# Attention transposes in the score slots' second banks, and the last two heads divided after the values

## The chip, the cores and the metric

The kernel runs on one core of a Trainium2 chip. The metric is the device time of one execution in microseconds. The core has a matrix engine (TensorE; PE in the profile, and PEld for its weight loads), a vector engine (DVE), a scalar engine (ACT) and a general engine (POOL). SyncE (SP) issues the transfers. Each engine works through its own instructions in a fixed order and waits on semaphores of the others. Matrix products land in PSUM, an accumulator memory that this kernel uses as eight banks of 512 fp32 numbers for each of 128 partitions.

## The reference, cut to what matters

The model is a two-layer trunk on a sequence of 1024 tokens with 1024 features: a forgetting attention, a SwiGLU block, a state-space mixer and another SwiGLU block, each between two RMS norms. The change touches the attention alone, which has 16 heads of 64 features:

```
for blk in range(seq_len // Q_BLOCK):            # 8 blocks of 128 queries
    s = jnp.einsum('bhqd,bhkd->bhqk', qb, kb).astype(jnp.float32) * scale
    s = s + c[:, :, q0:k_end, None] - c[:, :, None, :k_end]
    s = jnp.where(mask, s, -jnp.inf)
    p = jax.nn.softmax(s, axis=-1).astype(vb.dtype)
    outs.append(jnp.einsum('bhqk,bhkd->bhqd', p, vb))
o = o * jax.nn.sigmoid(gate)
return o @ w_out
```

The softmax is a quotient: the exponentials may be divided by their row sums before they meet the values, or the output of the values may be divided afterwards. Both give the same numbers up to rounding.

## The kernel before, in words

The attention is worked in **units**: one head `h` and one block of 128 queries `qb`. The blocks of a head run from 7 down to 0, and block `qb` sees `(qb + 1) * 128` keys, so the first four units of a head (qb 7 to 4) have more than 512 keys and the last four have 512 or fewer. There are 128 units.

**`scores(h, qb)`** (L542 on) adds the causal mask to one square of the bias tile on POOL (L547) and takes a score slot with `self.S("S")`. There are two slots, taken in turn, each of two PSUM banks: banks 0 and 1, banks 2 and 3. Unit i and unit i + 2 therefore have the same slot. TensorE fills it (L551 and L552, in pieces of 512 keys, so only units with qb of 4 or more write the second bank). DVE adds the bias in place and takes the row minimum (L555). ACT takes the exponential into an SBUF page `Pt` and the row sums into a column of `rs` (L561). For the last two heads (14 and 15, the pair called hp 7) DVE inverts the row sum (L563) and POOL multiplies the whole of `Pt` by it (L564).

**`transposes(h, qb)`** (L576 on) turns `Pt` over in squares of 128, up to four squares to a **group**: units with qb of 4 or more have two groups, the others one, so a head has 12 groups and a pair of heads 24. A group's squares are transposed by TensorE into one PSUM bank (L588), copied by ACT as the high part `pth` (L591) and subtracted by DVE to give the low part `ptl` (L592). The bank comes from `self.pb(PTB, ...)`. `PTB` has one entry, bank 6, so all groups of all units go through this bank, one after another.

**`values(h, j)`** (L594 on) multiplies two units' transposed squares with the values into bank 7 (L607). Every second time it copies and adds the two halves into the output page `o` (L611, L612). At a pair's end, for the pairs 0 to 6, POOL multiplies the page by a page of inverse sums (L614). Those come from **`sums(hp)`** (L566 on): the 16 columns of row sums are transposed through bank 6 (L569), inverted by DVE on 16 partitions (L570), written to DRAM and read back repeated over 64 partitions (L571, L573). Pair 7 has no such step.

**`attend`** strings the units together: in step i the scores of unit i, the transposes of unit i - 1 and, every second step, the values of two units before. **`fox`** weaves this stream with other matrix work of the same time: while the attention of pair hp runs, the projections q, k and v of pair hp + 1 and the gate of pair hp - 1 (L272 to L274, called `fm`) are handed out in shares. For hp 7 there are no projections left: what runs beside it is the gate of pair 6, the split of the first four output weights, the gate of pair 7 and the first tiles of `out_proj` (the same lines L272 to L274 with `woh` and `wol`). `out_proj` takes its accumulators with `self.S("pso")` from the same two slots.

The gate (L510 on) multiplies `o` with the sigmoid of the gate projection (L522). For pairs 0 to 6 the result goes to DRAM and comes back as the operand of `out_proj`. For pair 7 it stays in SBUF (`ogk`) and is split there (`wh`, `wl`, L253 and L254). It is the last of the eight k steps of each output tile.

The order of each engine's instructions is fixed when the kernel is built. A planner hands out the instructions by priority, which is their place in the program unless a block raises it (`high_priority(AHEAD)` around L555) or lowers it (the weight splits, L253 and L254). An instruction that the planner holds for not ready, by its own estimates of durations, is passed over, and a later one takes its place. So the transposes stand in the midst of `fm` products where the planner expects the bank to be free. Dependences in PSUM are kept bank by bank; the planner adds the semaphores.

Of the kernel before, what the change touches and what calls it, by code (L numbers as in the profile page):

```python
# [12 lines left out]
ALU = mybir.AluOpType  # L13

P = 128
D = 1024
NT = 8
NH = 16
HD = 64
# [12 lines left out]
PTB = (2,)  # L32
# [3 lines left out]
def f32(ap):  # L36
    return ap.bitcast(F32)
# [121 lines left out]
class Trunk:  # L159
# [369 lines left out]
    def attend(self, c, o):  # L529

        nc = self.nc
        units = [(h, qb) for h in range(NH) for qb in reversed(range(8))]
        An, pt, Pt, pv, rs, ri = {}, {}, {}, {}, {}, {}

        def load_bias(h):
            An[h] = self.R("An")
            nc.sync.dma_start(An[h], self.bcast(self.csum[h:h + 1, :], D))  # L540

        def scores(h, qb):  # L542
            qh, ql = c[h // 2]["q"][h % 2 * 2:h % 2 * 2 + 2]
            k = c[h // 2]["k"][h % 2]
            nk = (qb + 1) * P
            qs = slice(qb * P, nk)
            nc.gpsimd.tensor_add(An[h][:, qs], An[h][:, qs], self.cmask)  # L547
            ps = self.S("S")
            for c0 in range(0, nk, 512):
                c1 = min(c0 + 512, nk)  # L550
                nc.tensor.matmul(ps[:, c0:c1], qh[:, qs], k[:, c0:c1], start=True, stop=False)  # L551
                nc.tensor.matmul(ps[:, c0:c1], ql[:, qs], k[:, c0:c1], start=False, stop=True)  # L552
            with self.tc.high_priority(AHEAD):
                m = self.small("mx")
                nc.vector.tensor_tensor_reduce(out=ps[:, :nk], in0=ps[:, :nk], in1=An[h][:, :nk], op0=ALU.add, op1=ALU.min,  # L555
                                               scale=1.0, scalar=3e38, accum_out=m)
            p = Pt[h, qb] = self.R("Pt")
            if h // 2 not in rs:
                rs[h // 2] = self.small("rs", (P, 2, 8))
            r = rs[h // 2][:, h % 2, qb:qb + 1]  # L560
            nc.scalar.activation(p[:, :nk], ps[:, :nk], AF.Exp, bias=m, scale=-1.0, accum_out=r)  # L561
            if h >= NH - 2:
                nc.vector.reciprocal(r, r)  # L563
                nc.gpsimd.tensor_scalar(p[:, :nk], p[:, :nk], r, 1.0, op0=ALU.mult, op1=ALU.mult)  # L564

        def sums(hp):  # L566

            p2, r, x = self.pb(PTB, (P, P))[0:16], self.small("ri", (16, P)), self.R("RI")
            nc.tensor.transpose(p2, rs.pop(hp).rearrange("p a b -> p (a b)"), self.ident)  # L569
            nc.vector.reciprocal(r, p2)  # L570
            nc.sync.dma_start(self.ri_d[hp], r)  # L571
            for i in range(2):
                nc.sync.dma_start(x[i * 64:i * 64 + 64], self.bcast(self.ri_d[hp][i * 8:i * 8 + 8], D, 64))  # L573
            ri[hp] = x

        def transposes(h, qb):  # L576
            j, qq = qb // 2, qb % 2
            if qq:
                ng = (2 * j + 2 + 3) // 4
                pt[h, j] = [(self.R("pth", (P, 4, 256), F32R), self.R("ptl", (P, 4, 256), F32R)) for _ in range(ng)]  # L580
            p = Pt.pop((h, qb))
            for g in range(0, qb + 1, 4):
                n = min(4, qb + 1 - g)
                if g:
                    yield 0.11 * 4
                p2 = self.pb(PTB, (P, 4, P))
                for i in range(n):
                    nc.tensor.transpose(p2[:, i], p[:, (g + i) * P:(g + i + 1) * P], self.ident)  # L588
                th, tl = pt[h, j][g // 4]
                dh, dl = th[:, 0:n, qq * P:qq * P + P], tl[:, 0:n, qq * P:qq * P + P]  # L590
                nc.scalar.copy(dh, p2[:, 0:n])  # L591
                nc.vector.tensor_sub(dl, p2[:, 0:n], f32(dh))  # L592

        def values(h, j):  # L594
            h2, vt = h % 2, c[h // 2]["v"]
            if h2 == 0 and j == 3:
                o[h // 2] = self.R("o")
            r = slice(h2 * 64, h2 * 64 + 64)
            if j % 2:
                pv[h] = self.pb(PVB)  # L600
            out = pv[h][:, (j % 2) * 256:(j % 2) * 256 + 256]
            last = 2 * j + 1
            t = pt.pop((h, j))
            seq = [(0, 0)] + [(kb, i) for kb in range(1, last + 1) for i in (0, 1)] + [(0, 1)]
            for n, (kb, i) in enumerate(seq):
                lo = P if kb == last else 0
                nc.tensor.matmul(out[:, lo:], vt[kb // 4][:, kb % 4, h2, :], t[kb // 4][i][:, kb % 4, lo:],  # L607
                                 start=(n == 0), stop=(n == len(seq) - 1))
            if j % 2 == 0:
                d = o[h // 2][r, (j // 2) * 512:(j // 2) * 512 + 512]  # L610
                nc.scalar.copy(d, pv[h][64 - h2 * 64:128 - h2 * 64])  # L611
                nc.vector.tensor_add(d, d, pv[h][r])  # L612
                if h2 and j == 0 and h < NH - 2:
                    nc.gpsimd.tensor_mul(o[h // 2], o[h // 2], ri.pop(h // 2))  # L614

        load_bias(0)
        for i in range(len(units) + 3):
            hp = min(i, len(units) - 1) // 16
            if i < len(units):
                h, qb = units[i]  # L620
                if qb == 7:
                    yield 0.0, hp
                scores(h, qb)
                if qb == 2 and h + 1 < NH:
                    load_bias(h + 1)
                yield 0.16 * (qb + 1), hp
            if 1 <= i <= len(units):
                h, qb = units[i - 1]
                for x in transposes(h, qb):
                    yield x, hp  # L630
                yield 0.11 * (qb % 4 + 1), hp
                if h % 2 and qb == 0 and h < NH - 2:
                    sums(h // 2)
            if i >= 3 and (i - 3) % 2 == 1:
                h, qb = units[i - 3]
                values(h, qb // 2)
                yield 0.22 * (qb + 1), hp
# [1066 lines left out]
```

## Time and profile before

| | us |
|---|---|
| median of 3 runs | 2428.12 (2426.31 to 2430.02) |
| the profiled execution | 2426.33 |
| its span, first to last instruction | 2424.5 |
| attention, from the first scores (70.4) to the last values (669.7) | about 599 |
| one pair of heads, pairs 1 to 6 | 77.3 to 77.6 |

A profile page gives the busy time of each engine, the chain of work that ended last and the costliest groups of instructions. `L588` is line 588 of the kernel, `ps<-ident,Pt` says that `ps` is written from `ident` and `Pt`, and `x576` counts instructions. In a timeline a row begins with its start and its duration in us, and the part in brackets is the idle time of that engine just before it and what ended it. Matrix products are pipelined: the next one starts before the last has ended, so the time that a wait takes from TensorE is read from one start to the next. Weight loads (PEld) run ahead of the products, and a load that waits delays its product only by what the load was not ahead.

### The profile page before, as it was taken

What the parts mean: (1) busy time and instruction counts of PE and PEld (TensorE: products, weight loads), DVE (VectorE), ACT (ScalarE), POOL (GpSimd) and SP (SyncE); (2) the same over time, 40 slices, a digit from 0 to 9 for tenths busy, and PEclk for the clock granted to TensorE, in tenths of its full rate; (3) what the DMA queues carried; (4) which work ended last, traced back from release to release, by engine and by line L of the source; (5) the groups of instructions that cost most, each with busy time, mean ns of one, the idle gap of its engine ahead of it and who ended that gap; (6) DMA issues with size and microseconds to landing.
All of it is one profiled execution on the core that took longest, in us unless ns stands there. A gap on an engine that the chain in (4) does not pass through costs nothing.

```text
span 2424.5 us, 31559 instructions
## 1 busy us (share of the span) xinstructions
PE 2359.3 (97%) x11683; PEld 1938.8 (80%) x11683; DVE 1689.1 (70%) x2684; ACT 1204.4 (50%) x2029; POOL 455.2 (19%) x427
## 2 busy tenths in 40 slices
PE   7999999999999999999999999999999999999997
PEld 5777778777777888888878779888878888888886
DVE  6867776677678967666668686763795656555867
ACT  6766676667646333434564563232453333333334
POOL 4222222222400034545520001410000000000003
PEclk9999999999999999999999999999999999999999
DMA  4121112121243444343688752443424333237874
GB/s 146 48 61 53 49 48 62 53 61 54 87 149 101 121 127 135 117 136 116 204 293 301 270 170 84 135 147 107 135 80 135 107 98 109 92 118 261 284 239 157
DMA packets 252427, 318.23 MB, mean 131 GB/s; under 512 B 34225, under 2 KB 179937, under 8 KB 252273
## 3 DMA queue, kind: packets, MB, share of 16 engines
q1 hardware_dynamic: 252272, 316.23, 40.9%
q8 instruction: 91, 1.49, 0.3%
q14 instruction: 64, 0.52, 0.1%
HBM read 238.46 MB, written 77.72 MB: 130 GB/s over the span
## 4 chain that ended last, share of the span: by engine, by line
PE 74%; DVE 12%; ACT 7%; DMA 3%; issue 3%; POOL 0%; SPq 0%; DVEq 0%; ACTq 0%; POOLq 0%
PE ps L841 33%; PE ps L943 10%; PE ps L272 7%; PE ps L274 7%; PE ps L273 7%; PE ps L588 2%; PE ps L607 2%; DVE ps L555 1%; DMA raw<-in_ffn_w_down_dram 1%; DMA rot_d<-ry 1%; ACT wh L253 1%; PE ps L552 1%; PE ps L551 1%; DVE ptl L592 1%; DVE y L318 1%
## 5 line engine op out<-in xcount | busy, mean ns | idle before, releaser
L841 PE MATMUL ps<-B,ah 128*128 128x512 f32 x1056 | 326.0, 390 | 0.3 <-ACT B L89 0.3
L943 PE MATMUL ps<-wdh,gh 128*128 128x512 f32 x616 | 241.4, 392 | 6.3 <-ACT m L962 3.7
L943 PE MATMUL ps<-wdh,gl 128*128 128x512 f32 x616 | 240.9, 391 | 1.9 <-DVE gl L254 1.9
L943 PE MATMUL ps<-wdl,gh 128*128 128x512 f32 x616 | 240.9, 391 | 0.8 <-DVE wdl L254 0.8
L841 PEld LDWEIGHTS ps<-B,ah 128*128 128x128 f32 x1056 | 198.1, 188 | 42.7 <-ACT B L89 1.2
L841 PE MATMUL ps<-ops,ah 128*128 128x512 f32 x704 | 218.2, 391 | 0.0
L272 PE MATMUL ps<-hT,wh 128*128 128x512 f32 x512 | 207.5, 406 | 1.3 <-DVE pt L429 0.7
L841 PE MATMUL ps<-B,al 128*128 128x512 f32 x528 | 205.4, 389 | 0.0
L273 PE MATMUL ps<-hT,wh 128*128 128x512 f32 x512 | 204.4, 399 | 0.0
L274 PE MATMUL ps<-hT,wl 128*128 128x512 f32 x512 | 202.6, 396 | 0.0
L253 ACT CAST gh<-gr 128x1024 fp32r<-128x1024 f32 (+1 forms) x78 | 81.1, 1040 | 166.4 <-PE ps L943 138.0
L592 DVE TENSOR_TENSOR ptl<-ps,pth 128x512 fp32r<-128x512 f32 x192 | 106.4, 554 | 78.6 <-ACT pth L591 73.6
L254 DVE TENSOR_TENSOR gl<-gr,gh 128x1024 fp32r<-128x1024 f32 (+1 forms) x78 | 98.3, 1262 | 84.0 <-ACT gh L253 83.7
L841 PEld LDWEIGHTS ps<-ops,ah 128*128 128x128 f32 x704 | 131.5, 188 | 28.7 <-issue 1.7
L812 DVE TENSOR_TENSOR al<-raw,ah 128x1024 fp32r<-128x1024 f32 x88 | 117.1, 1333 | 50.5 <-ACT ah L811 50.5
L1655 POOL TENSOR_TENSOR y<-m,s 128x512 f32<-128x512 f32 x4 | 6.5, 1628 | 764.3 <-DVE wdl L254 759.5
L547 POOL TENSOR_TENSOR An<-An,cmask 128x128 f32<-128x128 f32 x128 | 80.2, 629 | 365.8 <-DVE mx L555 332.3
L811 ACT CAST ah<-raw 128x1024 fp32r<-128x1024 f32 x88 | 92.6, 1052 | 101.8 <-PE ps L841 99.4
L943 PEld LDWEIGHTS ps<-wdh,gh 128*128 128x128 f32 x616 | 116.3, 189 | 32.8 <-ACT m L962 4.2
L943 PEld LDWEIGHTS ps<-wdh,gl 128*128 128x128 f32 x616 | 116.2, 189 | 26.9 <-DVE gl L254 2.7
L841 PE MATMUL ps<-ops,al 128*128 128x512 f32 x352 | 136.9, 389 | 0.0
L943 PEld LDWEIGHTS ps<-wdl,gh 128*128 128x128 f32 x616 | 116.3, 189 | 25.5 <-DVE wdl L254 1.5
(358 smaller groups left out, 5867.2 us busy)
## 6 DMA issues: line engine op xcount, KB each, us to landing
raw<-in_ffn_w_down_dram SPq DMA_DIRECT2D x98, 512.0 KB, 5.2
gr<-g_d SPq DMA_DIRECT2D x76, 512.0 KB, 4.4
raw<-in_ffn_w_gate_dram SPq DMA_DIRECT2D x44, 512.0 KB, 4.1
raw<-in_ffn_w_up_dram SPq DMA_DIRECT2D x44, 512.0 KB, 4.8
g_d<-s SPq DMA_DIRECT2D x66, 256.0 KB, 2.2
raw<-in_fox_w_in_dram SPq DMA_DIRECT2D x32, 512.0 KB, 4.3
g_d<-up SPq DMA_DIRECT2D x22, 512.0 KB, 2.7
g_d<-up SPq DMA_DIRECT2D x44, 256.0 KB, 2.9
```

The source lines that it names most:

```text
L253: self.nc.scalar.copy(h, src)
L254: self.lsub.tensor_sub(l, src, f32(h))
L272: mm(ps, lh, rh, start=start, stop=False)
L273: mm(ps, lh, rl, start=False, stop=False)
L274: mm(ps, ll, rh, start=False, stop=stop)
L547: nc.gpsimd.tensor_add(An[h][:, qs], An[h][:, qs], self.cmask)
L588: nc.tensor.transpose(p2[:, i], p[:, (g + i) * P:(g + i + 1) * P], self.ident)
L592: nc.vector.tensor_sub(dl, p2[:, 0:n], f32(dh))
L811: nc.scalar.copy(h, src)
L812: V.tensor_sub(l, src, f32(h))
L841: nc.tensor.matmul(bank, x[:, k], y, start=start and k == i == 0, stop=True, skip_group_check=True)
L943: nc.tensor.matmul(bank, x[:, j, t], y[:, j], start=start and i == 0, stop=True, skip_group_check=True)
```

## The change

**Part one.** Each unit remembers the second bank of its score slot (`own`). The unit's first group of transposes goes into that bank if the unit has qb of 2 or more; second groups, and the single groups of qb 1 and 0, go through bank 6 as they did.

**Part two.** For heads 14 and 15 the inversion L563 and the POOL multiplication L564 are gone, and `sums` is called for pair 7 too. There it inverts the sums on 16 partitions as for the other pairs, but sends nothing to DRAM: POOL writes a selection matrix of ones and zeros (two copies, 16 partitions of 512 numbers each), and eight products of 128 x 128 spread the inverse sums over the 128 partitions into a score slot (`self.S("ri", ...)`, both banks). After the last values of head 15, DVE multiplies the page `o` by it out of PSUM. Since `ri` takes a turn of the two slots, the accumulators of `out_proj` that follow swap slots.

```diff
@@ attend, scores
             ps = self.S("S")
+            own[h, qb] = self.slots[self.nS % len(self.slots)] + 1
...
             nc.scalar.activation(p[:, :nk], ps[:, :nk], AF.Exp, bias=m, scale=-1.0, accum_out=r)
-            if h >= NH - 2:
-                nc.vector.reciprocal(r, r)
-                nc.gpsimd.tensor_scalar(p[:, :nk], p[:, :nk], r, 1.0, op0=ALU.mult, op1=ALU.mult)
@@ sums
             nc.vector.reciprocal(r, p2)
+            if hp == NH // 2 - 1:
+                sel, ri[hp] = x[0:16].rearrange("p (q f) -> p q f", f=P), self.S("ri", (P, 8, P))
+                for i in range(2):
+                    nc.gpsimd.tensor_copy(sel[:, :, i * HD:i * HD + HD],
+                                          self.ident[0:16, i * 8:i * 8 + 8, None].to_broadcast([16, 8, HD]))
+                for qb in range(8):
+                    nc.tensor.matmul(ri[hp][:, qb], sel[:, qb], r, start=True, stop=True)
+                return
@@ transposes
-            p = Pt.pop((h, qb))
+            p, b = Pt.pop((h, qb)), own.pop((h, qb))
...
-                p2 = self.pb(PTB, (P, 4, P))
+                p2 = self.bank(b, 1, (P, 4, P)) if not g and qb > 1 else self.pb(PTB, (P, 4, P))
@@ values
-                if h2 and j == 0 and h < NH - 2:
-                    nc.gpsimd.tensor_mul(o[h // 2], o[h // 2], ri.pop(h // 2))
+                if h2 and j == 0:
+                    if h < NH - 1:
+                        nc.gpsimd.tensor_mul(o[h // 2], o[h // 2], ri.pop(h // 2))
+                    else:
+                        nc.vector.tensor_mul(o[h // 2], o[h // 2], ri.pop(h // 2).rearrange("p a b -> p (a b)"))
@@ the loop over units
-                if h % 2 and qb == 0 and h < NH - 2:
+                if h % 2 and qb == 0:
                     sums(h // 2)
```

More of the change, by code (lines that the diff above doesn't have):

```diff
@@ L535, in attend @@
         units = [(h, qb) for h in range(NH) for qb in reversed(range(8))]
-        An, pt, Pt, pv, rs, ri = {}, {}, {}, {}, {}, {}
+        An, pt, Pt, pv, rs, ri, own = {}, {}, {}, {}, {}, {}, {}
         def load_bias(h):
```

## The prediction

> **What bounds the kernel now.** I read the profile's page first, then the sums of busy time by stretch, the waits of TensorE in the attention, and the timeline at the waits.
>
> ```profile
> span 2424.5 us, 31559 instructions
> PE 2359.3 (97%) x11683; PEld 1938.8 (80%) x11683; DVE 1689.1 (70%) x2684; ACT 1204.4 (50%) x2029; POOL 455.2 (19%) x427
> ```
> ```profile
> 448.20:525.66 77.46, 75.85 (x412) 61.51 (x410) 55.64 (x97) 53.47 (x102) 18.63 (x25) 1.00 0.19 55
> 603.00:672.00 69.00, 65.79 (x358) 51.14 (x359) 47.35 (x94) 45.72 (x85) 25.20 (x32) 1.00 0.35 104
> ```
>
> TensorE sets the pace: 97% of the span, 75.85 of 77.46 us in a middle pair of heads, at the full granted clock (1.00; the rows give stretch, length, and the busy time of PE, PEld, DVE, ACT and POOL). DVE (55.64) and ACT (53.47) have over 20 us to spare there. So a change pays only by what it takes from TensorE: work, or moments in which TensorE waits. These are its waits over the whole attention (60.5 to 672 us), the array's first, the weight loader's below, with the total, the count and the longest:
>
> ```profile
> PE ps L588 <- DVE ptl L592: 8.5, 22, 0.6
> PE ps L588 <- POOL Pt L564: 0.8, 2, 0.4
> PEld ps L588 <- DVE ptl L592: 39.9, 99, 1.1
> ```
>
> The largest is the transposes waiting for DVE's subtraction of the group before, that is, for bank 6 to come free. What one such wait costs is read from start to start:
>
> ```profile
> 465.24 0.39 PE L274 MATMUL ps<-hT,wl 128*128 128x512 f32 x1
> 465.47 0.39 PE L272 MATMUL ps<-hT,wh 128*128 128x512 f32 x1
> 466.14 0.55 PE L588 MATMUL ps<-ident,Pt 128*128 128x128 f32 x3 [0.29 <-DVE ptl L592]
> ...
> 468.84 0.39 PE L272 MATMUL ps<-hT,wh 128*128 128x512 f32 x1
> 469.32 0.66 PE L588 MATMUL ps<-ident,Pt 128*128 128x128 f32 x4
> ...
> 512.63 0.39 PE L272 MATMUL ps<-hT,wh 128*128 128x512 f32 x1
> 513.60 0.33 PE L588 MATMUL ps<-ident,Pt 128*128 128x128 f32 x1 [0.58 <-DVE ptl L592]
> ```
>
> A 512-column product takes the array 0.23 us (465.24 to 465.47). From 512.63 to 513.60 are 0.97, so 0.74 are lost where the row says 0.58; from 465.47 to 466.14 are 0.67, so 0.44 where it says 0.29. A counted wait costs its idle time and 0.16. At 468.84 to 469.32 0.25 us are lost with no idle time counted at all.
>
> In the last pair the bank is the chain itself:
>
> ```profile
> 656.61 0.69 DVE L592 TENSOR_TENSOR ptl<-ps,pth 128x512 fp32r<-128x512 f32 x1 [1.93 <-ACT pth L591]
> 658.19 0.29 DVE L592 TENSOR_TENSOR ptl<-ps,pth 128x128 fp32r<-128x128 f32 x1 [0.89 <-ACT pth L591]
> ...
> 657.36 0.33 PE L588 MATMUL ps<-ident,Pt 128*128 128x128 f32 x1 [0.22 <-DVE ptl L592]
> 658.63 0.63 PE L588 MATMUL ps<-ident,Pt 128*128 128x128 f32 x4
> ```
>
> The subtraction ends at 657.30, the next group starts at 657.36; it ends at 658.48, the next starts at 658.63. Transpose, copy and subtraction of one group follow each other, and the next group begins after them, while TensorE fills up with other products as long as there are any.
>
> **Part one, the second bank.** Of a head's 12 groups, 6 leave bank 6 (the first ones of qb 7 to 2). The 4 second groups and the 2 single ones stay, and each then has a whole unit between itself and the group before it in the bank. The first groups have nothing to wait for but their own exponential, which was the bank's last user. So I take all bank waits as removed: 8.5 + 22 x 0.16 = 12.0 us. Of the loader's 99 waits 77 have no counted wait of the array. One of these cost 0.25 (468.84 to 469.32); a dozen of that size, one or two for each pair, are 3.0, which I take. The bounds are 12.0, if all others are free, and 16, if each of the eight pairs has two. Together -15.0.
>
> It adds a wait. The second piece of the scores of unit i + 2 (qb 5 and qb 4 of each head, four in a pair; the later units of a head write the first bank only) now has to wait until DVE has subtracted the first group of unit i. Behind it in TensorE's queue stand `fm` products, the transposes of unit i + 1 and values, and DVE's minimum waits for it. Today these pieces sometimes run before that subtraction:
>
> ```profile
> 464.56 0.22 PE L551 MATMUL ps<-p,p 128*128 128x128 f32 x1
> ...
> 465.40 0.68 DVE L592 TENSOR_TENSOR ptl<-ps,pth 128x512 fp32r<-128x512 f32 x1
> ```
>
> Here the piece for qb 4 starts at 464.56 and the first group of qb 6 is done at 466.08: 1.5 us too early. The planner will put it later, behind `fm` products, but it misjudges a release by 0.25 to 0.74 us, as the waits above show. The bounds are nothing and four waits of 0.74 us for each of eight pairs, 23.7. I take one such wait for each pair, 8 x 0.74 = +5.9, because today five of 24 groups wait noticeably and only four pieces are exposed.
>
> **Part two, the division.** The removed work:
>
> ```profile
> L563 DVE RECIPROCAL rs<-rs x16: 145/160/180, 606.2 to 663.8; 128x1 f32<-128x1 f32 x16
> L564 POOL TENSOR_SCALAR Pt<-Pt,rs 128x1024 f32<-128x1024 f32 (+7 forms) x16 | 12.0, 749 | 24.2 <-DVE rs L563 23.7 <-PE ps L552 0.5
> ```
>
> 12.0 us of POOL and 2.5 of DVE go, neither of them the bound (25.20 and 47.35 of 69 us). What counts is that TensorE waited twice for the product: 0.8 + 2 x 0.16 = -1.1. About 0.9 us a unit between exponential and transposes go as well; beside the other products of TensorE they are worth nothing more.
>
> The added work, with the nearest rows:
>
> ```profile
> 688.36 1.09 PE ps L101 x8
> ...
> 1477.05 1.96 PE ps L1302 x32
> ...
> L570 DVE RECIPROCAL ri<-ps x7: 945/946/946, 143.6 to 608.5; 16x128 f32<-16x128 f32 x7
> 681.12 1.28 DVE L318 SCALAR_TENSOR_TENSOR y<-ps,rr,gn 128x1024 f32<-128x1024 f32 x1
> ```
>
> Eight fp32 products of 128 x 128: eight transposes of that size take 1.09 us, 32 products of half the output rows 1.96, that is 0.49 for eight. With the transpose of the sums I take +1.0 us of TensorE, bounds 0.5 and 1.2. POOL's two copies are bounded by the multiplication L564 (0.375 us at its smallest, 0.749 in the mean); they depend on nothing but a free page and lie under POOL's idle time; without that cover they would add up to 1.5 us ahead of the eight products. DVE gains an inversion of 0.95 us and a product out of PSUM, like L318: 1.28.
>
> Those two stand at the pair's end, where a chain leads to the last k step of `out_proj`:
>
> ```profile
> 669.33 0.38 PE L607 MATMUL ps<-ptl,vt 128*128 128x256 f32 x1
> ...
> 671.81 2.20 DVE L522 TENSOR_TENSOR ogk<-o,pt 128x1024 f32<-128x1024 f32 x1
> ...
> 674.39 0.50 PE L272 MATMUL ps<-woh,wh 128*128 128x512 f32 x1 [0.77 <-ACT wh L253]
> ```
>
> TensorE idles 0.77 us before the last k step at 674.39 and so loses 0.77 + 0.16 = 0.93 us. The inversion waits for bank 6 and so for the last subtraction, the eight products follow it, the new 1.28 us stand just before L522 (at 671.81), and the second accumulator of `out_proj` shares its slot with `ri`, so its products can't fill the gap until DVE has read it. If all of that were exposed: 0.95 + 1.09 + 1.28 = +3.3. If the shorter chain of the pair leaves TensorE with filling work to the end, the wait goes too: -0.9. I take +0.7, nearer the good end, because the transposes of the pair no longer queue for one bank and the work beside them is the same.
>
> POOL and DVE get in each other's way in this stretch:
>
> ```profile
> 617.21 2.40 POOL L614 TENSOR_TENSOR o<-o,RI 128x1024 f32<-128x1024 f32 x1
> 618.58 2.12 DVE L254 TENSOR_TENSOR wl<-raw,wh 128x1024 fp32r<-128x1024 f32 x1
> 662.06 1.23 DVE L254 TENSOR_TENSOR wol<-raw,woh 128x1024 fp32r<-128x1024 f32 x1 [0.39 <-ACT woh L253]
> ```
>
> The same split takes 2.12 us beside a POOL product and 1.23 alone. The Trainium skill, "SBUF — State Buffer", on the shared port pair, says that a DVE instruction with two SBUF inputs and a POOL instruction that reads SBUF exclude each other for the whole instruction; these rows agree. By that rule the two new POOL copies, if the planner puts them at the pair's end, would hold up L522 and so add up to 1.5 us there, and the 12.0 us of L564 would stop doing so to the weight splits. The sum above takes neither.
>
> **The sum.** -15.0 - 1.1 + 5.9 + 1.0 + 0.7 = -8.5 us. The profiled execution took 2426.33 us, of which the span is 2424.5; that gives 2417.8. It lies 1.8 under the median of the three runs, from which the same sum gives 2419.6. I say 2419.
>
> **The rivals.** A, the forecast: 5 to 14 us less. For it: the waits stand in every pair, and after the attention TensorE is busy again, so what is won is kept.
>
> B, the waits come back under other names: the planner, rid of one bank, puts the transposes earlier, up to the exponential, and the pieces of the scores wait instead. Two waits of 0.74 us for each pair give 11.8 instead of 5.9, the tail 3.3 instead of 0.7: -15.0 - 1.1 + 11.8 + 1.0 + 3.3 = 0.0, a time of 2428, 2423 to 2433. For it: TensorE's queue is fixed by estimates that miss. Against it: far fewer places can miss.
>
> C, slower: the second banks become the new chain. Scores, minimum, exponential, transposes, copy and subtraction of unit i must all end before unit i + 2 fills its second bank. If all four pieces of a pair wait as long as the longest wait of now, 4 x 8 x 0.74 = 23.7, and -15.0 - 1.1 + 23.7 + 1.0 + 0.7 = +9.3: 2437. It decides from the point where they cost more than 14.4 + 4.9 = 19.3 us in all, 2.4 us a pair. For it: the row at 464.56, 1.5 us early. Against it: the other pieces of that stretch would not have to move, and the planner has products to fill with in pairs 0 to 6.
>
> D, more than the forecast: the score waits are covered altogether (nothing instead of 5.9), and in the last pair, where TensorE is busy 65.79 of 69.00 us, the 3.2 idle us mostly go. -15.0 - 1.1 + 1.0 - 0.9 - 2 = -18.0: 2410. For it: the bank is the chain of that pair. Against it: each of its groups still needs scores, minimum and exponential first, and there is less to fill with.
>
> That the change doesn't do what it says, because the banks are held as one, is unlikely: the scores at 464.56 run although bank 6 is held until 466.08.
>
> **How the numbers follow.** A 0.48, D 0.16, B 0.22, C 0.14. About 0.2%, 4.9 us, is what a measurement of this kernel can tell from no change. Faster by more than that is A and D, 0.64; the same is B, 0.22; slower is C, 0.14. The range takes in A, most of D and the half of B next to A: 2409 to 2430, with some 0.06 left out below and 0.14 above. The forecast's own range is 2414 to 2423.
>
> **What would show it.** Right: in a pair of the middle the transposes' waits for DVE's `ptl` fall from 22 to a handful over the attention, the pair takes 76 instead of 77.5 us, and L551 or L552 show a few waits for `ptl`. The last pair's transposes no longer start within 0.15 us of a subtraction. The part behind 780 us looks as before, shifted. Wrong: the pair keeps its 77.5 us though the waits for the bank are gone (B), L551 waits for `ptl` by more than 2.4 us a pair (C), or TensorE idles over 2 us ahead of the first product with the last `wh` (the tail).

## The result and the profile after

The changed kernel takes 2414.45 us (median of 4 runs, 2413.52 to 2416.73) against 2428.11 for the kernel before on the same chip: a ratio of 0.9945, interval 0.9928 to 0.9962, that is 13.7 us less. In a later group of runs, on another chip, it took 2415.60 against 2425.83, a ratio of 0.9954 (0.9942 to 0.9967). The profiled execution took 2415.07. One execution of f2 below ran at a granted clock of 0.609 and took 3585.37 us; it is left out of every figure.

The page of the changed kernel, its span and its busy times:

```profile
span 2413.0 us, 31413 instructions
PE 2352.6 (97%) x11700; PEld 1947.3 (81%) x11700; DVE 1685.6 (70%) x2670; ACT 1200.6 (50%) x2029; POOL 447.9 (19%) x413
```

The sums by stretch, for pairs 0 to 6 (from 60.5 us to the first exponential of head 14), first of the kernel before, then of the changed one, whose second row is the pair of heads of the prediction's first row (columns: stretch, length, busy PE, PEld, DVE, ACT, POOL, granted clock, DMA share, GB/s):

```profile
60.50:605.00 544.50, 530.96 (x2859) 429.22 (x2858) 399.25 (x689) 380.04 (x728) 135.11 (x183) 1.00 0.18 54
```

```profile
60.50:592.30 531.80, 522.36 (x2860) 433.97 (x2859) 396.61 (x689) 376.45 (x728) 137.23 (x185) 1.00 0.19 55
439.06:514.73 75.67, 74.65 (x412) 62.18 (x410) 55.16 (x96) 52.93 (x102) 18.52 (x25) 1.00 0.19 56
```

The seven pairs are 12.7 us shorter with the same number of products (2859 and 2860). Only 4.1 us of that is idle time of TensorE (13.54 before, 9.44 after); 8.6 us were counted as busy. So part of the time that the products came late stands in the profile as work; the prediction's rows at 468.84 and 469.32 are such a place, with 0.25 us lost and no idle time. That is why the following table counts from start to start: the time from one product's start to the next, less its pace where nothing waits (0.227 us for 512 columns and in proportion, 0.109 for a transpose).

The change moves the lines of the kernel: L588 is now L595, L592 is L599, L561 is L562, and the two products of the scores, L551 and L552, are L552 and L553. TensorE's waits between 60 and 672 us, after (the array's, then the loader's; total, count, longest):

```profile
PE ps L595 <- DVE ptl L599: 2.8, 8, 0.4
PE ps L595 <- ACT Pt L562: 2.2, 9, 0.4
PE ps L552 <- DVE ptl L599: 1.5, 8, 0.3
...
PE ps L567 <- DVE ptl L599: 0.3, 1, 0.3
```

```profile
PEld ps L595 <- DVE ptl L599: 11.5, 21, 0.8
```

Before, transposes waited for their exponential only so much:

```profile
PE ps L588 <- ACT Pt L561: 0.6, 4, 0.2
```

Transposes that wait for the bank fell from 22 to 8 (the loader's from 99 to 21), the waits for POOL are gone, and two kinds are new or larger: scores (L552) that wait for the subtraction, and transposes (L595) that wait for their exponential. From start to start, in us, with the number of places where over 0.12 us were lost; but for the first and the last row, the rows are of pairs 0 to 6:

| | before | after |
|---|---|---|
| Pairs 0 to 6, length from 60 us on | 545.0 | 532.3 |
| transposes behind bank 6 (`ptl`) | 15.6 (37) | 5.4 (13) |
| transposes late otherwise, most by under 0.12 us each | 8.2 | 3.5 |
| transposes behind their exponential | 1.9 (6) | 2.8 (7) |
| scores behind `ptl` | 0 | 2.6 (8) |
| all losses | 52.5 | 39.6 |
| First exponential of head 14 to first `gate_up` product | 152.7 | 152.1, 150.2 |

In the last row the two figures of after are two executions, from the first and the later group of runs. Most of the difference is the granted clock. This is the first one, in four stretches of the sums:

```profile
638.00:640.00 2.00, 2.00 (x17) 1.88 (x17) 1.92 (x3) 1.71 (x3) 0.00 (x0) 1.00 0.96 258
640.00:641.00 1.00, 1.00 (x5) 0.81 (x5) 0.97 (x2) 0.00 (x0) 0.00 (x0) 0.81 0.91 262
641.00:644.20 3.20, 3.20 (x10) 2.51 (x9) 2.27 (x2) 0.49 (x1) 0.00 (x0) 0.53 0.96 348
644.20:646.00 1.80, 1.80 (x9) 1.49 (x8) 0.54 (x1) 1.41 (x3) 0.00 (x0) 1.00 0.95 317
```

The second execution over the same time:

```profile
640.00:646.00 6.00, 6.00 (x28) 4.96 (x27) 2.88 (x3) 1.57 (x2) 0.00 (x0) 1.00 0.84 302
```

In the first execution the clock was 0.81 and then 0.53 for 4.2 us in all, which costs 0.19 + 1.50 = 1.7 of the 1.9 us. So 150.2 is the number to compare: the end of the attention and `out_proj` gained 2.5 us, the whole attention with it 15.3 (the first `gate_up` product starts at 757.7 before and at 742.4 in the second execution).

The tail of the last pair, timeline of the first execution:

```profile
636.34 0.29 DVE L599 TENSOR_TENSOR ptl<-ps,pth 128x128 fp32r<-128x128 f32 x1 [1.08 <-ACT pth L598]
637.00 0.95 DVE L568 RECIPROCAL ri<-ps 16x128 f32<-16x128 f32 x1 [0.37 <-PE ps L567]
...
640.91 1.22 DVE L624 TENSOR_TENSOR o<-o,ps 128x1024 f32<-128x1024 f32 x1
...
652.99 2.17 DVE L522 TENSOR_TENSOR ogk<-o,pt 128x1024 f32<-128x1024 f32 x1 [1.76 <-ACT pt L519]
```

```profile
636.68 0.28 PE L567 MATMUL ps<-ident,rs 128*16 128x128 f32 x1 [0.35 <-DVE ptl L599]
...
638.00 2.05 PE L575 MATMUL ps<-ri,RI 16*128 16x128 f32 x16
639.97 0.50 PE L272 MATMUL ps<-hT,wh 128*128 128x512 f32 x1
```

The last values ended near 669.7 us before and end near 637.4 now, 32 us earlier, of which the shift of the seven pairs explains 12.7; 20 us the pair itself became shorter. That moved the end of `out_proj` by 2.5 us. And the eight products of the sums are 16 instructions (x16) that hold TensorE from 638.00 to 639.97.

### The profile page after: what moved, and what is told of

It reads as the page before. It is cut to its first block, busy times and chain, and to the rows that moved or that the text cites. A ratio compares the mean times of both kernels' runs of the same rounds, so it can differ in the third digit from the quotient of the medians.

```text
span 2413.0 us, 31413 instructions
## 1 busy us (share of the span) xinstructions
PE 2352.6 (97%) x11700; PEld 1947.3 (81%) x11700; DVE 1685.6 (70%) x2670; ACT 1200.6 (50%) x2029; POOL 447.9 (19%) x413
## 4 chain that ended last, share of the span: by engine, by line
PE 72%; DVE 12%; ACT 6%; DMA 4%; issue 4%; POOL 2%; SPq 0%; DVEq 0%; ACTq 0%; POOLq 0%
PE ps L851 31%; PE ps L953 11%; PE ps L272 7%; PE ps L274 7%; PE ps L273 7%; PE ps L595 2%; PE ps L614 1%; DMA raw<-in_ffn_w_down_dram 1%; DVE ptl L599 1%; PE ps L552 1%; DVE ps L556 1%; PE ps L553 1%; DMA rot_d<-ry 1%; ACT Pt L562 1%; ACT wh L253 1%
## 5 line engine op out<-in xcount | busy, mean ns | idle before, releaser
L599 DVE TENSOR_TENSOR ptl<-ps,pth 128x512 fp32r<-128x512 f32 x192 | 104.3, 552 | 50.2 <-ACT pth L598 47.9
```

## The experiments

The theories before the first four: W, the waits of TensorE for bank 6 in pairs 0 to 6 are the whole gain; D, the division carries a share of it; S, the score waits are the dear part of what is left. (This D is not the D of the prediction.) Later ones are named where they came up.

**e1, the banks alone.** The division of heads 14 and 15 stays ahead of the transposes:

```diff
             nc.scalar.activation(p[:, :nk], ps[:, :nk], AF.Exp, bias=m, scale=-1.0, accum_out=r)
+            if h >= NH - 2:
+                nc.vector.reciprocal(r, r)
+                nc.gpsimd.tensor_scalar(p[:, :nk], p[:, :nk], r, 1.0, op0=ALU.mult, op1=ALU.mult)
...
-                if h2 and j == 0:
+                if h2 and j == 0 and h < NH - 2:
...
-                if h % 2 and qb == 0:
+                if h % 2 and qb == 0 and h < NH - 2:
                     sums(h // 2)
```

> Part one alone: first groups in the second banks, heads 14 and 15 divided before the transposes as in the kernel before. Theory W (the gain is TensorE's waits for bank 6 in pairs 0 to 6, 12.7 us by the two traces, and the last pair gives next to nothing because TensorE has other products there): 2414 to 2417, within 2 us of the changed kernel, with the two waits of the transposes for POOL, 1.2 us, back. Rival D (the division of the last heads carries a share of its own, since the last pair's attention became 32 us shorter): 2418 to 2422.

Measured 2414.19 us, ratio 0.9942 (0.9929 to 0.9954): the whole gain, as W says. Pairs 0 to 6 take 532.1 us, and the stretch behind them 150.4 against 150.2. Its waits of TensorE, 60 to 672 us:

```profile
PE ps L598 <- POOL Pt L565: 3.2, 7, 0.9
PE ps L598 <- DVE ptl L602: 2.7, 7, 0.4
```

With the bank free, the multiplication on POOL is what the last pair's transposes wait for: 7 waits where there were 2, from start to start 4.65 us instead of 1.24. That is what the division in the output avoids, and its own products and waits cost as much.

**e2, the division alone.**

```diff
-                p2 = self.bank(b, 1, (P, 4, P)) if not g and qb > 1 else self.pb(PTB, (P, 4, P))
+                p2 = self.pb(PTB, (P, 4, P))
```

> Part two alone: all transposes through bank 6, heads 14 and 15 divided in the output. Theory W: pairs 0 to 6 as before at 77.5 us, the POOL waits of 1.2 us gone, 1.0 us of products added, the tail 0 to 2 us longer: 2427 to 2430, no change that can be told. Rival D: 2420 to 2424.

Measured 2429.95 us, ratio 1.0012 (1.0001 to 1.0023). Pairs 0 to 6 are those of before (544.8, transposes behind the bank 15.6 us), and the stretch behind is longer (155.8 against 152.7, of which a dip of the clock is some 1.7):

```profile
PE ps L595 <- DVE ptl L599: 9.2, 23, 0.8
...
PE ps L272 <- ACT woh L253: 0.9, 1, 0.9
```

The wait of the last k step, which the prediction had at 0.77 us, is still there under the new order. D falls: part two brings nothing by itself and is at best even.

**e3, both parts, but heads 14 and 15 in bank 6.**

```diff
-                p2 = self.bank(b, 1, (P, 4, P)) if not g and qb > 1 else self.pb(PTB, (P, 4, P))
+                p2 = self.bank(b, 1, (P, 4, P)) if not g and qb > 1 and h < NH - 2 else self.pb(PTB, (P, 4, P))
```

> Both parts, but the transposes of heads 14 and 15 stay in bank 6. Theory W: pairs 0 to 6 at 75.7 us, the last pair's attention long again by some 20 us, and the time still within 2 us of the changed kernel, 2414 to 2417, because other products fill TensorE. Rival D (the last pair's chain is worth what it became shorter): 2420 or more.

Measured 2417.57 us, ratio 0.9957 (0.9945 to 0.9970). Its stretch behind pair 6 is 155.3 us against 150.2, and again has 0.9 us ahead of a product with `woh`. By the times the second banks of the last pair are worth some 3 us (the intervals overlap), by the traces 5; without them the division in the output is dear. So W's "next to nothing" for the last pair holds only with the division of before.

**e4, second banks only for qb 5 to 2,** so that no second piece of scores has to wait for a subtraction:

```diff
-                p2 = self.bank(b, 1, (P, 4, P)) if not g and qb > 1 else self.pb(PTB, (P, 4, P))
+                p2 = self.bank(b, 1, (P, 4, P)) if not g and 1 < qb < 6 else self.pb(PTB, (P, 4, P))
```

> Second banks for the first groups of qb 5 to 2 only, so no piece of scores has to wait for a subtraction; the first groups of qb 7 and 6 are in bank 6 again. Theory W: the 3.3 us that TensorE lost at the scores of the changed kernel go, and waits at the second groups of qb 7 and 6 come back (0.44 us for a pair at one of them before, 3 us over the attention): 2413 to 2417, no difference. Rival S (the waits at the scores are the dear ones, since the planner holds back minimum and exponential behind them): 2409 to 2412.

Measured 2417.10 us, ratio 0.9959 (0.9945 to 0.9972): no better than the change, and pairs 0 to 6 take 538.7 us instead of 532.3. The score waits are gone, but the bank's are back:

```profile
PE ps L595 <- DVE ptl L599: 8.2, 21, 0.7
```

From start to start 13.7 us against 5.4. So the first groups of qb 7 and 6 are the ones whose bank matters, and 2.6 us of score waits are a small price for them. S falls, and W's 3 us for the waits that come back was too low: they are 8.3. (The times show less than the traces: the profiled execution of e4, 2414.76, is no slower than that of after, although its first `gate_up` product starts 5 us later. Behind that product the executions of these kernels take from 1664 to 1671 us.)

**e6, the sums in another slot.** The reciprocal sums stand in the slot that the second accumulator of `out_proj` needs. Here they go into the one that the last unit's scores used:

```diff
-                sel, ri[hp] = x[0:16].rearrange("p (q f) -> p q f", f=P), self.S("ri", (P, 8, P))
+                sel, ri[hp] = x[0:16].rearrange("p (q f) -> p q f", f=P), self.bank(self.slots[self.nS % 2], 2, (P, 8, P))
```

> The spread inverse sums go into the slot of the last unit and take no turn, so the accumulators of out_proj have the slots that they had before the change. Theory Q (the swap of the slots costs: the second accumulator waits until DVE has read the inverse sums): 2412 to 2413.5. Theory P (what costs is the products and their chain): no difference, 2413.5 to 2415.5.

Measured 2413.94 us, ratio 0.9947 (0.9934 to 0.9961), no difference; the stretch behind pair 6 takes 152.0 with the same dip of the clock at 640 us as the first execution of after (152.1). The shared slot costs nothing, because TensorE has products of the first accumulator and of other columns to fill with.

**e7, where the remaining waits are.** The 13 places of after are second groups of qb 4, which use bank 6 behind the second group of qb 5. The timeline of after at one of them:

```profile
500.37 0.40 PE L274 MATMUL ps<-hT,wl 128*128 128x512 f32 x1
500.69 0.41 DVE L599 TENSOR_TENSOR ptl<-ps,pth 128x256 fp32r<-128x256 f32 x1
...
501.16 0.33 PE L595 MATMUL ps<-ident,Pt 128*128 128x128 f32 x1 [0.39 <-DVE ptl L599]
```

The 256 columns subtracted at 500.69 are the second group of qb 5; the single transpose of qb 4 starts 0.06 us after their end. That subtraction in its turn is late because its copy needs a page of `pth`, which the values of the unit pair before give back: the group's transposes ended at 494.06, and its copy began at 498.95, 0.05 us after the signal of a product that reads `pth` (L614). In each of the heads 0 to 13 the last signal that this copy waits for is one of L614, and the copy begins 4.4 to 5.6 us after the transposes. No run gives `pth` another page. Theory M was that freeing this place would only move the wait, to the scores of qb 2. The edit puts this group into the first bank of the unit's own slot, which the exponential has freed:

```diff
-                p2 = self.bank(b, 1, (P, 4, P)) if not g and qb > 1 else self.pb(PTB, (P, 4, P))
+                p2 = self.bank(b, 1, (P, 4, P)) if not g and qb > 1 else self.bank(b - 1, 1, (P, 4, P)) if g and qb == 4 else self.pb(PTB, (P, 4, P))
```

> The second group of qb 4, one square, goes into the first bank of its unit's slot instead of bank 6. In the changed kernel TensorE still loses 0.24 to 0.56 us there in each head, because the group of qb 5 before it in bank 6 holds the bank until a page of pth is free. Theory W (each wait for a bank that goes is TensorE's gain): 0.8 us for each of seven pairs less, 2408.5 to 2411. Rival M (the wait moves to the scores of qb 2, which need that first bank): 2413 to 2416.

Measured 2408.06 us, ratio 0.9924 (0.9911 to 0.9937), some 5 to 6 us better than the change. Its waits of TensorE:

```profile
PE ps L595 <- ACT Pt L562: 3.8, 11, 0.9
PE ps L454 <- ACT pt L461: 2.1, 6, 1.0
PE ps L552 <- DVE ptl L599: 1.5, 8, 0.3
...
PE ps L595 <- DVE ptl L599: 0.2, 1, 0.2
```

From start to start the transposes behind the bank fall from 5.4 to 0.2 us, those behind the exponential rise from 2.8 to 3.9 and L454 behind ACT from 2.4 to 3.3; pairs 0 to 6 take 527.1 us instead of 532.3. The wait moved in small part, and not to the scores. M falls, and W's 0.8 us for each pair holds (0.7).

**e8, what the division costs in either form.** This kernel leaves out a part of the computation: heads 14 and 15 are not divided by their sums at all.

```diff
-                if h2 and j == 0:
+                if h2 and j == 0 and h < NH - 2:
...
-                if h % 2 and qb == 0:
+                if h % 2 and qb == 0 and h < NH - 2:
                     sums(h // 2)
```

> The changed kernel with the division of heads 14 and 15 left out altogether (their outputs stay undivided), which prices each way of dividing. Theory P (each way costs TensorE time in the last pair: 1.0 us of products, 0.85 us of waits around them and about 1 us behind them in the changed kernel; 4.6 us of waits for POOL where the exponentials are multiplied): 2410 to 2412.5. Rival F (TensorE fills with other products whatever the last pair does): 2413.5 to 2415.5, like the changed kernel and like the second banks alone.

Measured 2407.84 us, ratio 0.9925 (0.9913 to 0.9938), 6 us under the change by the medians and less than either theory had. The traces show less: the stretch behind pair 6 takes 148.9 us against 150.2 (after) and 150.4 (e1). The rest is at least in part the clock: the mean granted clock over its five executions is 0.9958 and over those of after 0.9945, and 0.0013 of 2408 us are 3.1. So the division costs some 1.4 us by the traces and about 3 by the times brought to one clock, in either form; in an execution with the drop of the clock at 640 us, 1.7 more in the changed kernel. The difference between the 1.4 and the 3 is not settled.

**f1, head 14 divided by way of DRAM, head 15 as before.** Head 14's sums take the way of the other pairs (transpose, reciprocal, DRAM, multiplication on POOL), since only head 15 is at the very end. The diff is cut to its core:

```diff
+            if h == NH - 1:
+                nc.vector.reciprocal(r, r)
+                nc.gpsimd.tensor_scalar(p[:, :nk], p[:, :nk], r, 1.0, op0=ALU.mult, op1=ALU.mult)
...
+        def sums14(hp):
+            p2, r, x = self.pb(PTB, (P, P))[0:8], self.small("ri", (16, P))[0:8], self.R("RI")
+            nc.tensor.transpose(p2, rs[hp][:, 0], self.ident)
+            nc.vector.reciprocal(r, p2)
+            nc.sync.dma_start(self.ri_d[hp][0:8], r)
+            nc.sync.dma_start(x[0:64], self.bcast(self.ri_d[hp][0:8], D, 64))
+            ri[hp] = x
...
+                elif h == NH - 2 and j == 0:
+                    nc.gpsimd.tensor_mul(o[h // 2][r], o[h // 2][r], ri.pop(h // 2)[r])
```

> Second banks; head 14 is divided in its output on POOL by inverse sums that go through DRAM like those of the pairs before (half a page, while head 15 runs), head 15 before its transposes. Theory P: half of the 4.6 us of POOL waits of the second banks alone go and nothing is added at the end: 2411 to 2413. Rival F: 2413.5 to 2415.5.

Measured 2412.11 us (2407.63 to 2414.55), ratio 0.9937 (0.9924 to 0.9951). Its stretch takes 148.7 us, as short as without any division, with two waits for POOL left (1.7 us) and no products of sums. By the times alone it can't be told from the change.

**f2, e7 and f1 together; f3, the same and also the single groups of qb 1 and 0 in second banks** (`not g` in place of `not g and qb > 1`). They ran beside the changed kernel on one chip.

> The two edits that helped, together: the second group of qb 4 in its slot's first bank, and head 14 divided in its output through DRAM while head 15 is divided before its transposes. If TensorE's waits in pairs 0 to 6 (5 us) and in the last pair (2 to 3 us) are separate stretches of one queue, the gains add: 2404 to 2407, 20 to 24 us under the kernel before. If the one takes the place of the other: 2407 to 2410.

> As the one above, with the single groups of qb 1 and 0 in the second banks too, so bank 6 is left with the second groups of qb 7 to 5. The scores of the next head's qb 7 and 6 are exposed then. TensorE loses 0.15 us a pair at qb 0 today; four more pieces of a pair may wait 0.3 us each: 2404 to 2414, no better than the one above and up to 7 us worse.

> The changed kernel once more, on the same chip as the two above, so that they can be compared with it directly: 2412 to 2416.

| | us, median | ratio to before (interval) | pairs 0 to 6 | behind, to `gate_up` |
|---|---|---|---|---|
| changed kernel | 2415.60 | 0.9954 (0.9942 to 0.9967) | 532.2 | 150.2 |
| f2 | 2407.73 | 0.9925 (0.9912 to 0.9937) | 527.4 | 151.3 |
| f3 | 2413.20 | 0.9947 (0.9934 to 0.9960) | 531.2 | 153.0, of which a drop of the clock 1.7 |

f2 is 7.9 us better than the change, but no better than e7 alone: the gain of f1 is not there. Waits of f2, then of f3:

```profile
PE ps L606 <- POOL Pt L565: 2.6, 4, 1.4
...
PE ps L552 <- DVE ptl L610: 1.1, 6, 0.2
```

```profile
PE ps L606 <- POOL Pt L565: 3.2, 3, 2.1
PE ps L606 <- ACT Pt L562: 2.9, 9, 0.9
PE ps L552 <- DVE ptl L610: 2.7, 13, 0.3
```

In f2, with the bank out of the way, head 15's transposes wait for the multiplication on POOL again (5 places, 3.5 us from start to start, against 1.7 in f1). In f3 the scores wait in 15 places instead of 8 (5.0 us against 2.6): the single groups had hardly waited in bank 6 (0.14 us a pair at qb 0), so their second bank brings little but the price. e7 and f2 are the fastest kernels here that compute everything, 18 to 19 us under the kernel before.

## Why the prediction was right, and where it was off

The forecast, 2419 us, has the sign and the mechanism, and the 2414.45 lies at the low end of its own range (2414 to 2423). Its gain was nearly 5 us too small. Step by step, in us from start to start, before against the undisturbed execution of after:

- **Bank waits, -15.0.** Measured -15.0 in pairs 0 to 6 (15.6 to 5.3, and 8.2 to 3.5 for the smaller amounts) and about -0.5 in the last (0.9 to 0.4). The size is right, but by two errors that cancel. The 22 waits are 37 places from start to start in pairs 0 to 6 alone, and there was more to win than 12 + 3. And the sentence that failed is the one that each second group has "a whole unit between itself and the group before it in the bank": for the second group of qb 4 that unit is not enough, because the subtraction of qb 5's second group, behind its late copy (e7), ends only just before it. 5.3 us stayed, and e7 wins them.
- **Score waits, +5.9.** One for each pair was nearly right in number (8, and 3 in the last pair), the size was not: +2.6 and +0.8, about 0.3 us each and not 0.74. The price came from the longest wait of the transposes; the scores' longest idle time is 0.3.
- **Not foreseen: transposes behind their exponential,** +0.9 in pairs 0 to 6 and +0.9 in the last. The prediction said that first groups wait for nothing else, and did not price that wait. It is of the kind that B described, but small.
- **POOL, -1.1.** Measured -1.2. But measured against e1 the multiplication would have cost 4.65 once the banks were there. A term priced from the trace of before held only for that kernel.
- **Added products, +1.0, bounds 0.5 and 1.2.** Both bounds failed: the eight products are 16 instructions, 0.123 us each, 1.97 together, besides the transpose of the sums. Transposes were the wrong nearest row: each of these products is issued as two instructions and takes 0.246 us. The Trainium skill, "FP8 and Floating Point Precision", section "TensorE Precision Notes", says that a true FP32 product takes four passes through the array. An estimate from that page at the pace of this kernel's products (0.227 us for 512 columns, so 0.057 for 128) is 4 x 0.057 = 0.23 us, and the trace agrees within a tenth. Read beside the prediction's rows, it would have put the term at 1.8.
- **POOL's two copies.** Hidden, as said, and far from the tail:

```profile
L572 POOL COPY RI<-ident x2: 607/1614/2622, 536.7 to 539.2; 16x512 f32<-16x512 f32 x2
```

 They ran 100 us ahead of the pair's end, since their page was free, so they could not hold up the last pair's L522, which takes 2.17 us against 2.20. But they ran beside the L522 of pair 5, and one of the two took 2.62 us, the other 0.61:

```profile
536.34 2.47 DVE L522 TENSOR_TENSOR pt<-o,pt 128x1024 f32<-128x1024 f32 x1 [1.54 <-POOL o L622]
536.66 3.18 POOL L572 COPY RI<-ident 16x512 f32<-16x512 f32 x2
```

 The first copy ends 0.48 us after L522 does, and so in all seven executions that have these copies. The prediction's price (up to 1.5 us for both) holds for a copy alone, not for one beside L522, and it was POOL that waited and not DVE: L522 took 2.47 us, like the others of its line (2.39 to 2.50 in pairs 0 to 4). The rule on the shared port pair that the prediction cites, of the Trainium skill's page "SBUF — State Buffer", agrees with that.
- **Tail, +0.7.** Measured -0.1: the transpose of the sums behind the last subtraction 0.57, the products behind the reciprocal 0.28, and the wait of the last k step gone, -0.94, as the good end of the bounds had it. The multiplication on DVE and the shared slot (e6) cost nothing.
- **The last pair.** The "3.2 idle us mostly go" of the prediction's D was nearer than the forecast, which had no term for it: products behind ACT's copies and exponentials, and transposes late for no cause that the profile names, lost 3.4 us before; what stands there after is one product of the values that loses 0.9 behind a subtraction. That is about -2.5. But the pair became 20 us shorter for that; while TensorE has other products, the length of a chain is no time.

These terms and the two for the exponentials add up to about -12. The rest, about -3 us, is spread over neighbours of the transposes and many small places (the `fm` products of pairs 0 to 6 lost 12.2 us before and 10.4 after); no run takes it apart. Together the attention and `out_proj` gained 15.3 us, and the times say 13.7.

C fell: the scores' waits are 3.4 us, not 23.7. B fell: the pair takes 75.7 us and not 77.5. "The part behind 780 us looks as before, shifted" holds for the work but not for its time. In the first execution two groups of products waited for POOL in `gate_up`, by the waits of L1229 (L1219 before; the array's and the loader's counted together):

```profile
  POOL s5w L1215: 3.2, 4
  issue: 2.8, 8
```

In the second execution of the same kernel they did not, and e1 has none either; e6 and e3 have 2.0 and 1.5 us of it, and the kernel before 0.4. That is a difference between executions, and no effect of the change.

## What to carry to other kernels

Where TensorE sets the pace, count what a wait costs from start to start of its products: here 8.6 of the 12.7 us that were won stood in the profile as busy time. When a buffer's waits are to be removed, follow each user of it one step further than the buffer: the group that still waited for bank 6 stood behind a copy that waited for a page, two steps away, and moving just that group won another 40% of what the change had won (532.3 to 527.1 us against 545.0 to 532.3). And price a removed wait against the kernel that will be there, not against the one before: POOL's multiplication cost 1.2 us behind one bank and 4.7 behind two.

## What was not expected of the hardware

The granted clock drops to half several times in each execution, and at some places only in some: at 640 us in one execution of the changed kernel and in e6, but not in the other execution. A drop lasts 3.41 us or twice that, and while TensorE is busy it costs half its length, so one execution's stretch can differ by 1.7 us from another's of the same code, as 152.1 and 150.2 did. This is the drop at 640 us with the 3.41 us ahead of it, both of the first execution, and one of double length of the kernel before:

```profile
637.20:640.61 3.41, 3.30 (x23) 2.65 (x23) 3.33 (x4) 2.51 (x4) 0.00 (x0) 1.00 0.97 261
640.61:644.02 3.41, 3.41 (x10) 2.67 (x9) 2.63 (x3) 0.31 (x1) 0.00 (x0) 0.50 0.98 341
```

```profile
1266.69:1273.52 6.83, 5.84 (x13) 4.15 (x14) 6.79 (x11) 4.28 (x7) 0.00 (x0) 0.50 0.89 323
```

The Trainium skill, "TensorE: Matmul & The Clock Gate", describes a gate that halves the clock after the array has been idle for a window of 3.4 us. The length and the depth agree, but not the idle array. Leaving out the end of each execution, TensorE was busy for up to 57% of the 3.41 us ahead of a drop in the 13 traces, and in three cases for more: 97% in the row above, 97% in e6 at 641 us and 94% in e2 at 673 us. These three stand behind the thin products of the sums, which use 16 of 128 rows of the array. Those products fill 60% of the 3.41 us there; without them TensorE was busy for 36 to 39%.

Seven of the 13 executions have these products, and four of them show no drop there. In each trace the drops begin whole multiples of 3.41 us apart, so the windows are known: in three of the four (the second execution of after, e3 and e4) the products fall into two windows, and in e7 they leave 44% to other products. No such window at the full clock, from 30 us on, in which TensorE was busy for less than 43% passed without a drop behind it. So the traces fit a gate that hardly counts the thin products as work. No run gives these products more rows, so this is not shown. The drop of f3 at 630 us, without such products, is of the common kind (38% busy).

Brought to full clock (each execution's time by its mean granted clock, which is recorded to three decimals, so this is an estimate to about a us), the means are 2414 for before, 2401.5 for the change, 2400.4 for e1, 2417.2 for e2, 2404.6 for e3, 2405.2 for e4, 2398.4 for e8 and for f1, 2395.6 for e7 and 2395.5 for f2. That is nearly the order of the medians, but e8 stands behind e7 and f2, with less between the change and e8.
